# 1/rms by rounded parts, positions behind the low parts, one factor at the end, and a gate moved: four edits to a decoder block on one core

## The chip, the core and the metric

The kernel runs on one core of one Trainium2 chip. The core has a matrix engine (PE, TensorE, whose weight loads the profile shows as PEld), a vector engine (DVE), a scalar engine (ACT), GpSimd (POOL) and a queue for transfers (SP). Each engine works off its own list of instructions in order, and they wait for each other through semaphores. The metric is device time in microseconds (us), the median of three runs of the whole program. All times below are us unless marked ns.

## The reference

One decoder block on 512 tokens of width 1024, in float32. Cut to what matters here:

```python
xn = rmsnorm(x, norm_mix_g)
proj = xn @ w_in     # q latent 384, kv latent 256 + rotary key 32, diff q 512, diff k 512, diff v 512, gates 2 x 1024
# branch A: latent attention, 8 heads (latents normed, projected up, rotary on 32 dims)
# branch B: differential attention, 4 heads of two maps each
o_diff = rmsnorm(softmax(q1 k1) v - lam * softmax(q2 k2) v, g) * (1 - lambda_init)
merged = sigmoid(gate_a) * (o_mla @ w_branch_mla) + sigmoid(gate_b) * (o_diff @ w_branch_diff)
x = x + merged @ w_out
x = x + (silu(hn @ w_gate) * (hn @ w_up)) @ w_down      # hn = rmsnorm(x), hidden width 2816
return rmsnorm(x, norm_final_g)
```

Rotary angles are position times frequency; the kernel turns them into sine and cosine itself.

## The kernel before

**Rounded parts.** Most products on PE are of a rounded float32 format (F32R); line 521 is the one 512-column product of plain float32. To keep accuracy the kernel splits most operands in a high part (rounded, by ACT or DVE) and a low part (the rest, by DVE) and adds three products: high by high, high by low, low by high (`mm3`, lines 299 to 301). Every weight tile is loaded by SP into one of four `raw` buffers (`weights`, line 268), ACT rounds it (line 261) and DVE subtracts (line 266) into one of three `w` buffers. Products gather in PSUM accumulators: three named `mm`, two `sc` (scores), two `tr` (transposes), one `pv` (values).

**Order.** The program is written in a natural order, and a planner puts each engine's instructions in order: it follows a model of their times, takes what is ready by priority, and gives out buffers as they come free. Three priorities are set by hand: attention (`urgent`) goes ahead of the remaining work, and the first reading of a product (`feed`) goes ahead of both. `tc.issue_after(x)` puts an instruction behind `x` on the same engine. The remaining work is filling between the steps of attention; the lists `FILL`, `FILL_MLA` and `FILL_DIFF` (lines 46 to 54) say in which order. An entry is a gate product (24 matmuls of 512 columns, line 468, read out at line 481), `qk` (q and k of a differential head, 24 such matmuls each, lines 568 to 589), `v` (half of the differential values, four groups of 24 matmuls of 256 columns, line 594), or a part of branch A. `FILL_DIFF[0]` stands ahead of differential head 0 in the program.

**Stages.** (1) The start: transposed x, 128 of its 1024 columns at a time, and the latent weights come in; ACT makes the high parts (lines 344, 349) and DVE the low parts (345, 350), while PE multiplies (`latent`). `last_hi` and `last_lo` chain these on ACT and DVE. The positions come over ACT's queue; DVE turns them into angles (401 to 403) and reduces these to parts of a turn (405 to 421), ACT takes sines (433). (2) 1/rms of each token, `x_rs` (four columns of 128 tokens), comes from sums of squares. The gates and the differential q and k have tokens along the free dimension, so they need it as a row repeated on all partitions, `x_rms`: DVE scales an identity by each column (`diag`, 519), PE multiplies a matrix of ones by it (521), DVE copies the result (523). The first gate (line 524) and the cosine and sine tables (538, 540) are multiplied by it. (3) Latents, up-projections, and attention with filling. In `rotate` (555) DVE reads the accumulator twice (shuffle 558, product 559), after which it is free; POOL does the rest (560, 561). (4) Sigmoids, branch and output projections, FFN. (5) The down projection gathers 512 of 1024 output columns for four rows of tokens at a time. `finish` (924) adds the residual (929), ACT sums squares (930), POOL multiplies by the gain (931). After the second half, ACT makes y, an approximate 1/rms, DVE one correction factor z (937, 938), and each half of the row is multiplied by y and by z: the second half on DVE in one instruction (941), the first by y on ACT (940) and by z on DVE (943). SP stores both.

Of the kernel before, what the change touches and what calls it, by code (L numbers as in the profile page):

```python
# [13 lines left out]
F32R = mybir.dt.float32r  # L14
BF16 = mybir.dt.bfloat16
I32 = mybir.dt.int32
AF = mybir.ActivationFunctionType
ALU = mybir.AluOpType
# [3 lines left out]
P = 128  # L22
S = 512
D = 1024
KD = D // P
NB = S // P
# [21 lines left out]
            [("mqk", 2), ("mr", 2), ("gate", 0, 3), ("gate", 0, 4), ("mv", 1)],  # L48
            [("mqk", 3), ("mr", 3), ("qk", 0)],
            [("qk", 1)]]  # L50
FILL_DIFF = [[("qk", 2), ("v", 1)],
             [("qk", 3), ("gate", 0, 5), ("gate", 0, 6)],
             [("gate", 0, 7), ("gate", 1, 0), ("gate", 1, 1)],
             [("gate", 1, m) for m in range(2, KD)]]
PBUFS = dict(mm=3, sc=2, tr=2, pv=1)
# [33 lines left out]
def build(ctx, nc, tc, a, out):  # L89
    sb = ctx.enter_context(tc.tile_pool(name="sb", bufs=1))  # L90
# [8 lines left out]
    def T(tag, shape, dtype):  # L99
        return sb.tile(shape, dtype, name=nm(tag), tag=tag, bufs=BUFS[tag])  # L100

    def PS(tag):
        return pp.tile([P, 512], F32, name=nm("ps_" + tag), tag=tag, bufs=PBUFS[tag])
# [7 lines left out]
    def tmp():  # L111
        return T("t", [P, S], F32)

    def sm(w=1):
        return T("sm", [P, w], F32)

    def r32(ap):
        return ap.bitcast(F32)

    def dma(o, i):  # L120
        nc.sync.dma_start(out=o, in_=i)
# [19 lines left out]
    def urgent():  # L141
        return attention
# [14 lines left out]
    def log_exp(**kw):  # L157
        with tc.issue_after(table[0].ins):
            return nc.scalar.activation(**kw)  # L159
# [12 lines left out]
            nc.tensor.matmul(out=warm_ps, lhsT=warm[:, :P], rhs=warm, start=True, stop=True)  # L172
    ones = sb.tile([P, P], F32, name="ones")
    nc.vector.memset(ones, 1.0)

    misc = T("PT", [P, 2560], F32)

# [14 lines left out]
    ang, turn, pos_i, ah = [misc[:, i * P:(i + 1) * P] for i in (6, 7, 8, 10)]  # L192
    pos_i, ah = pos_i.bitcast(I32), ah.bitcast(F32R)
# [18 lines left out]
    for t in range(NB):  # L212
# [4 lines left out]
                            scalar2=None, op0=ALU.mult)  # L217

    ident = sb.tile([P, P], F32, name="ident")
# [8 lines left out]
    def rsqrt(ss, n, w=1):  # L228

        v, y, z = sm(w), sm(w), sm(w)  # L230
        nc.vector.tensor_scalar(out=v, in0=ss, scalar1=1.0 / n, scalar2=EPS, op0=ALU.mult, op1=ALU.add)
        log_exp(out=y, in_=v, func=AF.Ln)
        last_exp[0] = log_exp(out=y, in_=y, func=AF.Exp, scale=-0.5)
        if w == 1:
            nc.vector.tensor_scalar(out=z, in0=v, scalar1=y, scalar2=y, op0=ALU.mult, op1=ALU.mult)
        else:
            nc.vector.tensor_mul(out=z, in0=y, in1=y)
            nc.vector.tensor_mul(out=z, in0=z, in1=v)
        nc.vector.tensor_scalar(out=z, in0=z, scalar1=-0.5, scalar2=1.5, op0=ALU.mult, op1=ALU.add)
        nc.vector.tensor_mul(out=y, in0=y, in1=z)  # L240
        return y
# [14 lines left out]
    last_hi, last_lo = [None], [None]  # L256
# [69 lines left out]
    lat_mm = [None]  # L326
# [57 lines left out]
    x_rs = rsqrt(x_ss, D, NB)  # L384
# [13 lines left out]

    nc.vector.tensor_copy(out=ang, in_=pos_i)
    nc.vector.tensor_scalar(out=ang, in0=ang, scalar1=ccol[:, 0:1], scalar2=0.0, op0=ALU.mult, op1=ALU.add)
    nc.vector.tensor_copy(out=ah, in_=ang)
    ahl, acc, ry, rx = [v[:, c:c + 2 * P].rearrange("p (s n) -> p s n", s=2) for v in (tmp(), tmp()) for c in (0, 2 * P)]
    with tc.issue_after(last_lo[0].ins):
        nc.vector.tensor_copy(out=ahl[:, 0, :], in_=r32(ah))
    nc.vector.tensor_sub(out=ahl[:, 1, :], in0=ang, in1=ahl[:, 0, :])
    for j, c in enumerate(_inv_2pi_pieces()):
        nc.vector.tensor_scalar(out=ry, in0=ahl, scalar1=c, scalar2=MAGIC, op0=ALU.mult, op1=ALU.add)
# [18 lines left out]
    for src in (turn_c, turn):  # L428
        tg = tmp()
        nc.gpsimd.memset(tg, 0.0)  # L430
        for q in range(4):
            with tc.issue_after(last_sin.ins):
                last_sin = nc.scalar.activation(out=tg[32 * q:32 * q + 32, q * P:(q + 1) * P],
                                                in_=src[32 * q:32 * q + 32, :], func=AF.Sin, scale=TWO_PI)
# [57 lines left out]
    qk = {}  # L492

    def fill(work):
        for kind, *args in work:
            if kind == "gate":
                gate(*args)
            elif kind == "v":
                diff_v(*args)
            elif kind == "qk":  # L500
                qk[args[0]] = diff_qk(*args)
            elif kind == "pe":
                pe[args[0]] = mla_pe(*args)
            elif kind == "mv":
                mv[args[0]] = mla_v(*args)
            elif kind == "mqk":
                mqk[args[0]] = mla_qk(*args)
            elif kind == "mr":
                mla_rope(args[0], mqk[args[0]], pe[args[0] // 2])
# [4 lines left out]
    latent_out(1, pss)  # L514

    ps = PS("mm")
    diag = tmp()
    for t in range(NB):
        nc.vector.tensor_scalar(out=diag[:, t * P:(t + 1) * P], in0=ident, scalar1=x_rs[:, t:t + 1], scalar2=None, op0=ALU.mult)
    with tc.issue_after(lat_mm[0].ins):  # L520
        nc.tensor.matmul(out=ps, lhsT=ones, rhs=diag, start=True, stop=True)
    x_rms = sb.tile([P, S], F32, name="x_rms")
    nc.vector.tensor_copy(out=x_rms, in_=ps)
    gate(0, 0, first_gate)
# [141 lines left out]
        return ps  # L666


    ones_r = sb.tile([P, P], F32R, name="ones_r")
    nc.vector.tensor_copy(out=ones_r, in_=ones)  # L670
    eps = sb.tile([P, 1], F32, name="eps")
    nc.gpsimd.memset(eps, EPS)

# [137 lines left out]
    for h in range(4):  # L811
        parts_first[0] = True
        fill(FILL_DIFF[h])
        with urgent():
# [50 lines left out]
    for t, half in ((0, 0), (1, 0), (0, 1), (1, 1), (2, 0), (2, 1), (3, 0), (3, 1)):  # L865
        xs = x1[t][:, half * S:(half + 1) * S]
        ps = PS("mm")
# [16 lines left out]
    for f, n in products[:3]:  # L884
        w = weights(kview(n, f * P, P), KD, P)
        ps = PS("mm")
# [4 lines left out]
    for n_, (f, n) in enumerate(products):  # L891
        if n_ < 3:
            ps, w = early[n_]
            ffn_product(ps, w, 256, 512)
        else:
            w = weights(kview(n, f * P, P), KD, P)
            ps = PS("mm")
# [26 lines left out]
    def finish(t, c0, c1, ps):  # L924

        xs = x1[t][:, c0:c1]
        g = g_fin[c0 // S][:, c0 % S:c0 % S + c1 - c0]
        ss, b = sm(), sm()
        nc.vector.tensor_add(out=xs, in0=xs, in1=ps)
        nc.scalar.activation(out=tmp()[:, :c1 - c0], in_=xs, func=AF.Square, accum_out=ss)  # L930
        nc.gpsimd.tensor_mul(out=xs, in0=xs, in1=g)  # L931
        nc.vector.tensor_scalar(out=b, in0=ss, scalar1=1.0 / D, scalar2=base.get(t, EPS), op0=ALU.mult, op1=ALU.add)
        if c1 == D:
            y, z = sm(), sm()
            log_exp(out=y, in_=ss, func=AF.Ln, scale=1.0 / D, bias=base[t])
            log_exp(out=y, in_=y, func=AF.Exp, scale=-0.5)
            nc.vector.tensor_scalar(out=z, in0=b, scalar1=y, scalar2=y, op0=ALU.mult, op1=ALU.mult)
            nc.vector.tensor_scalar(out=z, in0=z, scalar1=-0.5, scalar2=1.5, op0=ALU.mult, op1=ALU.add)
            xs, x0 = x1[t][:, S:D], x1[t][:, 0:S]
            nc.scalar.activation(out=x0, in_=x0, func=AF.Copy, scale=y)  # L940
            nc.vector.tensor_scalar(out=xs, in0=xs, scalar1=y, scalar2=z, op0=ALU.mult, op1=ALU.mult)
            dma(out[0, t * P:(t + 1) * P, S:D], xs)
            nc.vector.tensor_scalar(out=x0, in0=x0, scalar1=z, scalar2=None, op0=ALU.mult)
            dma(out[0, t * P:(t + 1) * P, 0:S], x0)
        base[t] = b

    for half in range(2):
        acc = [PS(t_) for t_ in (("mm", "mm", "mm", "sc") if half == 0 else ("sc", "tr", "tr", "pv"))]

        def down(t, w, k0):  # L950
            for k in range(2):
                mm3(acc[t], [hid[k0 + k][s][:, t * P:(t + 1) * P] for s in range(2)],
                    [w[s][:, k, :] for s in range(2)], k0 + k == 0, k0 + k == NF - 1)

        last = []
        for k0 in range(0, NF, 2):
            w = weights(kview("w_ffn_down", half * S, S, k0, 2), 2, S)
            if half == 1 and k0 >= NF - 6:
                last.append((w, k0))
                continue  # L960
            for t in range(NB):
                down(t, w, k0)
        for t in range(NB):
            for w, k0 in last:
                down(t, w, k0)
            for c0, c1 in (((0, LAST), (LAST, S)) if half == 1 and t == NB - 1 else ((0, S),)):
                finish(t, half * S + c0, half * S + c1, acc[t][:, c0:c1])
# [32 lines left out]
```

## Time and profile before

| what | value |
|---|---|
| three runs | 740.13, 741.04, 740.1; median 740.13 |
| the profiled execution, its own time | 740.23 |
| span from first to last instruction in it | 738.5 |
| mean granted PE clock | 0.999 |

The span of the profiled execution is 1.7 shorter than its own time; the rest lies around the span. The profile has these views: a page with busy times, the chain that ended last and the costliest groups; waits (who waited for whom); a timeline of instructions (start, duration, engine, line, operation, output and inputs, shapes, count, and in brackets idle time ahead of it with what ended it); and busy time by stretches. Matmuls overlap and their ends are modelled, so a step from one start to the next says more than a duration.

### The profile page before, as it was taken

Reading aid. Unit: us, or ns where it says so; the run is one execution under the profiler, and the core shown is the slowest. Engines: PE = TensorE matmul, PEld = TensorE weight load, DVE = VectorE, ACT = ScalarE, POOL = GpSimd, SP = SyncE. Lnnn points to the kernel's source line nnn. Section 1 sums busy time; section 2 is a strip of 40 time slices with the busy share of each in tenths; the row PEclk is TensorE's granted clock in tenths of the full one; section 3 lists DMA queues with packets and bytes.
Section 4 is the critical chain, followed back from the end, with each engine's and each line's share of the span. In section 5 each row is a group of like instructions: output and inputs, shape, how many; then the busy total and the mean of one; then the engine's idle time right before and its main releaser. Section 6 shows DMA issues by size and latency. Waiting matters only on the chain.

```text
span 738.5 us, 9543 instructions
## 1 busy us (share of the span) xinstructions
PE 729.0 (99%) x3602; PEld 617.2 (84%) x3602; DVE 413.6 (56%) x812; ACT 333.7 (45%) x613; POOL 48.4 (7%) x45
## 2 busy tenths in 40 slices
PE   9999999999999999999999999999999999999996
PEld 7978988888888888888898888888888888888885
DVE  7789789988898765793634333333233232222514
ACT  7765678676766526561433223223232231212314
POOL 1000000322041101000000000000000000000303
PEclk9999999999999999999999999999999999999999
DMA  9615455323433312346204233332333323223203
GB/s 335 196 59 138 120 129 137 93 59 85 115 86 86 114 59 87 114 161 210 84 3 143 86 108 92 90 110 86 105 94 88 112 86 102 98 88 113 86 1 114
DMA packets 100414, 78.82 MB, mean 107 GB/s; under 512 B 6416, under 2 KB 87056, under 8 KB 100368
## 3 DMA queue, kind: packets, MB, share of 16 engines
q1 hardware_dynamic: 100080, 78.13, 35.9%
q8 instruction: 28, 0.46, 0.3%
q14 instruction: 18, 0.15, 0.1%
q10 hardware_dynamic: 288, 0.08, 0.0%
HBM read 71.91 MB, written 2.10 MB: 100 GB/s over the span
## 4 chain that ended last, share of the span: by engine, by line
PE 96%; DVE 3%; ACT 0%; issue 0%; DVEq 0%
PE ps_mm L299 25%; PE ps_mm L300 25%; PE ps_mm L301 25%; PE ps_sc L627 3%; PE ps_tr L653 2%; PE ps_tr L301 2%; PE ps_sc L300 2%; PE ps_sc L299 2%; PE ps_sc L301 2%; PE ps_tr L299 2%; PE ps_tr L300 2%; PE ps_pv L774 1%; PE ps_pv L664 1%; PE ps_pv L301 1%; PE ps_pv L300 1%; PE ps_pv L299 1%
## 5 line engine op out<-in xcount | busy, mean ns | idle before, releaser
L261 ACT ACTIVATE w<-raw 128x1024 fp32r<-128x1024 f32 (+3 forms) x110 | 109.4, 998 | 253.5 <-issue 150.7
L266 DVE TENSOR_TENSOR w<-raw,w 128x1024 fp32r<-128x1024 f32 (+3 forms) x114 | 133.7, 1175 | 159.8 <-ACT w L261 159.5
L299 PE MATMUL ps_mm<-X,w 128*128 128x512 f32 (+1 forms) x568 | 217.3, 383 | 0.1
L300 PE MATMUL ps_mm<-X,w 128*128 128x512 f32 (+1 forms) x568 | 216.8, 382 | 0.0
L301 PE MATMUL ps_mm<-X,w 128*128 128x512 f32 (+1 forms) x568 | 216.4, 381 | 0.0
L299 PEld LDWEIGHTS ps_mm<-X,w 128*128 128x128 f32 x568 | 106.7, 188 | 20.4 <-issue 0.3
L300 PEld LDWEIGHTS ps_mm<-X,w 128*128 128x128 f32 x568 | 106.9, 188 | 20.0 <-issue 0.2
L301 PEld LDWEIGHTS ps_mm<-X,w 128*128 128x128 f32 x568 | 106.8, 188 | 20.0
L905 DVE TENSOR_TENSOR t<-t,ps_mm 128x512 f32<-128x512 f32 x22 | 15.1, 688 | 66.8 <-PE ps_mm L301 66.1
L159 ACT ACTIVATE P<-P,sm 128x128 f32<-128x128 f32 (+3 forms) x64 | 35.7, 558 | 21.4 <-DVE sm L631 21.0
L931 POOL TENSOR_TENSOR L<-L,P 128x512 f32<-128x512 f32 (+1 forms) x9 | 12.6, 1421 | 434.8 <-ACT t L930 434.8
L627 PE MATMUL ps_sc<-L,L 96*128 96x128 f32 (+7 forms) x160 | 37.3, 327 | 0.2 <-DVE sm L631 0.2
L300 PE MATMUL ps_mm<-w,L 128*128 128x512 f32 (+1 forms) x100 | 37.3, 373 | 0.0
L299 PE MATMUL ps_mm<-w,L 128*128 128x512 f32 (+1 forms) x100 | 37.1, 373 | 0.0
L301 PE MATMUL ps_mm<-w,L 128*128 128x512 f32 (+1 forms) x100 | 37.0, 373 | 0.0
L300 PE MATMUL ps_mm<-L,w 128*128 128x512 f32 x90 | 35.4, 394 | 0.0
L299 PE MATMUL ps_mm<-L,w 128*128 128x512 f32 x90 | 35.4, 395 | 0.0
L301 PE MATMUL ps_mm<-L,w 128*128 128x512 f32 x90 | 35.1, 390 | 0.0
L631 DVE CUSTOM_DVE_ANT_0 P<-ps_sc,mask 128x128 f32<-128x128 f32 (+3 forms) x64 | 30.5, 477 | 5.8 <-PE ps_sc L627 5.0
L246 ACT ACTIVATE L<-t 64x512 fp32r<-64x512 f32 (+2 forms) x47 | 29.2, 621 | 6.9 <-PE ps_pv L301 3.7
L627 PEld LDWEIGHTS ps_sc<-L,L 96*128 96x128 f32 (+1 forms) x160 | 26.7, 189 | 3.3 <-DVE sm L631 0.4
L250 DVE TENSOR_TENSOR L<-t,L 128x512 fp32r<-128x512 f32 (+2 forms) x37 | 26.3, 711 | 3.5 <-ACT L L246 3.1
(271 smaller groups left out, 1136.8 us busy)
## 6 DMA issues: line engine op xcount, KB each, us to landing
raw<-w_in SPq DMA_DIRECT2D x28, 512.0 KB, 4.0
raw<-w_ffn_gate SPq DMA_DIRECT2D x22, 512.0 KB, 3.9
raw<-w_ffn_up SPq DMA_DIRECT2D x22, 512.0 KB, 3.9
raw<-w_ffn_down SPq DMA_DIRECT2D x22, 512.0 KB, 3.6
L<-x SPq DMA_DIRECT2D x8, 512.0 KB, 7.3
L<-L SPq DMA_DIRECT2D x32, 128.0 KB, 3.7
raw<-w_out SPq DMA_DIRECT2D x8, 512.0 KB, 3.9
L<-xt SPq DMA_DIRECT2D x8, 256.0 KB, 4.4
```

Of the source, the lines that this page charges most:

```text
L159: return nc.scalar.activation(**kw)
L246: nc.scalar.activation(out=hi, in_=src, func=AF.Copy, scale=scale)
L250: nc.vector.tensor_sub(out=lo, in0=src, in1=r32(hi))
L261: nc.scalar.activation(out=o, in_=i, func=AF.Copy)
L266: (nc.vector if w_eng[1] == 'dve' else nc.gpsimd).tensor_sub(out=o, in0=i, in1=r32(hi))
L299: nc.tensor.matmul(out=o, lhsT=lh, rhs=rh, start=start, stop=False)
L300: nc.tensor.matmul(out=o, lhsT=lh, rhs=rl, start=False, stop=False)
L301: return nc.tensor.matmul(out=o, lhsT=ll, rhs=rh, start=False, stop=stop)
L627: nc.tensor.matmul(out=ps[:, :n], lhsT=q[:, i * P:n], rhs=k[:, 0:n], start=j == 0, stop=j == last)
L631: nc.vector.tensor_tensor_reduce(out=m, in0=ps[:, :n], in1=mask[:, S - n:], scale=-1.0, scalar=3.4e38, op0=ALU.add, op1=ALU.min, accum_out ...
L653: nc.tensor.transpose(out=ps[:, c:c + P], in_=blocks[i][:, j * P:(j + 1) * P], identity=ident)
L905: nc.vector.tensor_mul(out=g, in0=g, in1=ps)
```

## The change

Four edits. 1/rms as a row: `x_rs` is split in a rounded part and the rest, each gives a diagonal, and two products with a rounded matrix of ones (`ones_r`, now made at the start) replace the one product of plain float32. Positions: the copy that begins the angles is put behind the last low part (`last_lo`), and the rounded copy of the angles behind it follows by its inputs. The end: DVE multiplies y and z once into yz; each half of the row is multiplied by yz, the first on ACT, which also issues the store of it on its own queue, the second on DVE, stored by SP. Filling: gate 5 of the first branch moves from the second list of `FILL_DIFF` to the head of the first one, ahead of `qk 2`.

```diff
-FILL_DIFF = [[("qk", 2), ("v", 1)],
-             [("qk", 3), ("gate", 0, 5), ("gate", 0, 6)],
+FILL_DIFF = [[("gate", 0, 5), ("qk", 2), ("v", 1)],
+             [("qk", 3), ("gate", 0, 6)],
              [("gate", 0, 7), ("gate", 1, 0), ("gate", 1, 1)],
...
+    ones_r = sb.tile([P, P], F32R, name="ones_r")
+    nc.vector.tensor_copy(out=ones_r, in_=ones)
...
-    nc.vector.tensor_copy(out=ang, in_=pos_i)
+    with tc.issue_after(last_lo[0].ins):
+        nc.vector.tensor_copy(out=ang, in_=pos_i)
...
-    with tc.issue_after(last_lo[0].ins):
-        nc.vector.tensor_copy(out=ahl[:, 0, :], in_=r32(ah))
+    nc.vector.tensor_copy(out=ahl[:, 0, :], in_=r32(ah))
...
-    diag = tmp()
-    for t in range(NB):
-        nc.vector.tensor_scalar(out=diag[:, t * P:(t + 1) * P], in0=ident, scalar1=x_rs[:, t:t + 1], scalar2=None, op0=ALU.mult)
-    with tc.issue_after(lat_mm[0].ins):
-        nc.tensor.matmul(out=ps, lhsT=ones, rhs=diag, start=True, stop=True)
+    x_hi, x_lo = sm(NB), sm(NB)
+    nc.vector.tensor_copy(out=x_hi.bitcast(F32R), in_=x_rs)
+    nc.vector.tensor_sub(out=x_lo, in0=x_rs, in1=x_hi)
+    for j, part in enumerate((x_hi, x_lo)):
+        diag = tmp().bitcast(F32R)
+        for t in range(NB):
+            nc.vector.tensor_scalar(out=diag[:, t * P:(t + 1) * P], in0=ident, scalar1=part[:, t:t + 1], scalar2=None,
+                                    op0=ALU.mult)
+        with tc.issue_after(lat_mm[0].ins):
+            nc.tensor.matmul(out=ps, lhsT=ones_r, rhs=diag, start=j == 0, stop=j == 1)
...
-            nc.scalar.activation(out=x0, in_=x0, func=AF.Copy, scale=y)
-            nc.vector.tensor_scalar(out=xs, in0=xs, scalar1=y, scalar2=z, op0=ALU.mult, op1=ALU.mult)
+            nc.vector.tensor_mul(out=yz, in0=y, in1=z)
+            nc.scalar.activation(out=x0, in_=x0, func=AF.Copy, scale=yz)
+            nc.scalar.dma_start(out=out[0, t * P:(t + 1) * P, 0:S], in_=x0)
+            nc.vector.tensor_scalar(out=xs, in0=xs, scalar1=yz, scalar2=None, op0=ALU.mult)
             dma(out[0, t * P:(t + 1) * P, S:D], xs)
-            nc.vector.tensor_scalar(out=x0, in0=x0, scalar1=z, scalar2=None, op0=ALU.mult)
-            dma(out[0, t * P:(t + 1) * P, 0:S], x0)
```

More of the change, by code (lines that the diff above doesn't have):

```diff
@@ L666, in values @@
         return ps
-    ones_r = sb.tile([P, P], F32R, name="ones_r")
-    nc.vector.tensor_copy(out=ones_r, in_=ones)
     eps = sb.tile([P, 1], F32, name="eps")
@@ L933, in finish @@
         if c1 == D:
-            y, z = sm(), sm()
+            y, z, yz = sm(), sm(), sm()
             log_exp(out=y, in_=ss, func=AF.Ln, scale=1.0 / D, bias=base[t])
```

## The prediction, made before the result was known

> **What bounds the kernel now.** I read the head of the page first, then TensorE's own waits, then a table by stretches of time, and last the single instructions around each hole.
>
> ```profile
> span 738.5 us, 9543 instructions
> PE 729.0 (99%) x3602; PEld 617.2 (84%) x3602; DVE 413.6 (56%) x812; ACT 333.7 (45%) x613; POOL 48.4 (7%) x45
> ...
> PE 96%; DVE 3%; ACT 0%; issue 0%; DVEq 0%
> ```
>
> The last row is the chain that ended last: 96% of it is TensorE (PE). So only two things can shorten the run: fewer PE columns, or the holes in which PE waits. The 3% of VectorE (DVE) says where to look for the holes. TensorE's waits name one, and the table by stretches shows the stage that it lies in (columns: busy time and count of PE, PEld, DVE, ACT, POOL, then granted clock, DMA share and GB/s).
>
> ```profile
> PE ps_mm L299 <- DVE t L559: 0.9, 1, 0.9
> ```
>
> ```profile
> 160.00:177.00 17.00, 17.00 (x113) 15.69 (x113) 13.38 (x33) 12.51 (x27) 3.79 (x4) 1.00 0.39 94
> 177.00:196.00 19.00, 17.69 (x108) 14.95 (x108) 18.74 (x47) 14.24 (x32) 5.68 (x4) 1.00 0.25 58
> ...
> 276.00:731.00 455.00, 454.97 (x2092) 379.94 (x2091) 179.95 (x233) 145.78 (x210) 13.77 (x9) 1.00 0.32 97
> ```
>
> From 276 on PE is never without work, so what is gained or lost ahead of it arrives at the end in full. Between 177 and 196 DVE is busy 18.74 of 19 us and PE is not. That is where differential head 0 runs, with the third head's q and k (line 51, `qk 2`) and the second value half (`v 1`) as filling. The instructions:
>
> ```profile
> 42.11 0.40 PE L301 MATMUL ps_mm<-X,w 128*128 128x512 f32 x1
> 42.34 0.39 PE L299 MATMUL ps_mm<-X,w 128*128 128x512 f32 x1
> ...
> 167.11 0.39 PE L301 MATMUL ps_mm<-X,w 128*128 128x512 f32 x1
> ...
> 179.45 0.28 PE L653 MATMUL ps_tr<-ident,P 128*128 128x128 f32 x1
> 179.91 0.44 PE L627 MATMUL ps_sc<-L,L 128*128 128x128 f32 x2 [0.18 <-DVE sm L631]
> 181.21 0.39 PE L299 MATMUL ps_mm<-w,X 128*128 128x256 f32 x1 [0.86 <-DVE t L559]
> ...
> 193.73 0.51 PE L627 MATMUL ps_sc<-L,L 128*128 128x384 f32 x2
> 194.46 0.82 PE L664 MATMUL ps_pv<-PT,L 128*128 128x512 f32 x2 [0.22 <-ACT PT L246]
> 195.33 0.50 PE L299 MATMUL ps_mm<-X,w 128*128 128x512 f32 x1
> ```
>
> ```profile
> 179.85 0.74 DVE L558 STREAM_SHUFFLE t<-ps_mm 128x512 f32<-128x512 f32 x1
> 180.48 0.68 DVE L559 TENSOR_TENSOR t<-ps_mm,tab 128x512 f32<-128x512 f32 x1
> ...
> 181.72 0.67 DVE L559 TENSOR_TENSOR t<-ps_mm,tab 128x512 f32<-128x512 f32 x1
> ```
>
> The ends of matmuls are modelled, so I use starts. A 512-column matmul starts 0.23 after the one before it (42.11 to 42.34), a 128-column one by that scale 0.06. The step from 179.45 to 179.91 is 0.46 instead of 0.06, hole A of 0.40. From 179.91 to 181.21 pass 1.30 instead of 0.12, hole B of 1.18. At 193.73 two of 384 columns should take 0.34 and take 0.73; at 194.46 one of 512 and one of 384 should take 0.40 and take 0.87: hole C, 0.39 + 0.47 = 0.86. The reason of B is in the rows: the k product of `qk 2` was complete at 167.11, yet its rotation (L558, L559), which frees the accumulator, ends at 182.39, 15 us later, and that of q ends at 181.16. The three `mm` accumulators are then q, k and the first half of `v 1`; the second half starts at 181.21, when q's is read out.
>
> **Part 1, 1/rms by rounded parts.** Removed: one 128x512 product of plain float32. Added: two of rounded parts, and on DVE a rounding copy, a subtraction and four more diagonal blocks.
>
> ```profile
> 40.78 1.02 PE L521 MATMUL ps_mm<-t,ones 128*128 128x512 f32 x2
> ...
> 41.87 0.40 PE L300 MATMUL ps_mm<-X,w 128*128 128x512 f32 x1
> ```
>
> From 40.78 to 41.87 pass 1.09; the one ordinary matmul left out between them is 0.23 of that, so L521 costs 0.86. Two rounded products, by the ordinary step, cost 2 x 0.23 = 0.46, a saving of 0.40 on PE. Whether it arrives depends on DVE:
>
> ```profile
> 34.13 0.17 DVE L386 TENSOR_TENSOR sm<-sm 128x4 f32<-128x4 f32 x1
> ...
> 34.41 0.28 DVE L519 TENSOR_SCALAR t<-ident,sm 128x128 f32<-128x128 f32 x1
> 36.17 0.43 DVE L436 CAST P<-t 128x512 fp32r<-128x512 f32 x1 [1.48 <-ACT t L433]
> ...
> 47.33 0.69 DVE L481 TENSOR_TENSOR L<-ps_mm,x_rms 128x512 f32<-128x512 f32 x1 [0.71 <-PE ps_mm L301]
> ```
>
> ```profile
> 49.89 0.47 PE L299 MATMUL ps_mm<-L,w 128*128 128x512 f32 x1
> 50.46 0.66 PE L460 MATMUL ps_tr<-ident,L 128*128 128x128 f32 x4
> ```
>
> By the first two rows the addition is 2 x 0.17 + 4 x 0.28 = 1.5 us at most, nearer 1.2 where such instructions overlap. Two idle times cover it: 1.48 ahead of L436, if the blocks are placed there, and 0.71 ahead of L481. PE stands 0.34 at 49.89 (0.57 instead of 0.23) at the end of the DVE work that L481 begins, so the saving lives only if L481 starts earlier too. Bounds: -0.4 with DVE covered, +0.5 if all 1.2 falls behind 36.17 and only 0.7 is covered. I take -0.3, near the first, because 2.2 of cover stand against 1.2.
>
> **Part 2, positions behind the low parts.** Three small DVE instructions leave the start and run just ahead of the angle reduction.
>
> ```profile
> 4.45 0.23 DVE L401 CAST PT<-PT 128x128 f32<-128x128 int32 x1 [0.46 <-DMA PT<-positions]
> ...
> 5.18 0.75 DVE L345 SCALAR_TENSOR_TENSOR X<-L,cols,X 128x512 fp32r<-128x512 f32 x1
> ...
> 29.51 0.17 DVE L231 TENSOR_SCALAR sm<-sm 128x4 f32<-128x4 f32 x1 [1.83 <-ACT L L379]
> ```
>
> From L401 to the first low part (L345) pass 0.73, and the low parts move up by about that; but PE is still on high parts then and has no wait there among its waits. Where they go, the angle chain ends ahead of an idle 1.83, and 0.7 fits. I cost it at 0; if the cover were gone it would be +0.7 of DVE time with the 0.71 ahead of L481 still behind it. No DMA moves.
>
> **Part 3, one factor at the end.**
>
> ```profile
> 732.17 0.42 ACT L930 ACTIVATE t<-L 128x256 f32<-128x256 f32 x1 [1.71 <-DVE L L929]
> ...
> 733.73 0.72 ACT L940 ACTIVATE L<-L,sm 128x512 f32<-128x512 f32 x1
> 733.98 0.15 DVE L938 TENSOR_SCALAR sm<-sm 128x1 f32<-128x1 f32 x1
> 734.24 0.55 DVE L941 TENSOR_SCALAR L<-L,sm,sm 128x512 f32<-128x512 f32 x1
> 734.70 0.48 DVE L943 TENSOR_SCALAR L<-L,sm 128x512 f32<-128x512 f32 x1
> 734.82 0.81 SPq L121 DMA_DIRECT2D out<-L  x2
> ```
>
> ```profile
> 736.00:736.50 0.50, 0.00 (x0) 0.00 (x0) 0.00 (x0) 0.00 (x0) 0.00 (x0) 1.00 0.98 369
> ```
>
> The product y*z (0.17, by L386, with its wait 0.2) comes ahead of both scalings. The one-factor form takes 0.48 instead of 0.55, so the first store leaves some 0.1 later. ACT's copy of the other half no longer runs under z but behind y*z: 734.45 to 735.17, and its store is issued then, about where SP issues its second one today (734.82 plus half of 0.81). The DMA engines are at a share of 0.98 while both stores drain, so the end follows the first store: +0.1. For the earlier rows of tokens ACT now also spends some 0.4 per store issue, and its Square of the next rows (L930) is queued behind. Before the last L930 ACT idles 1.71; a copy some 0.65 later plus 0.4 fits. Bounds: -0.4 (one issue time, if the issue were what delays the last store) and +0.5 (an ACT that comes late to L930).
>
> [...]
>
> **Part 4, a gate ahead of `qk 2`.** The sum of PE work is unchanged: 24 matmuls of 0.23, 5.5 us, move from behind `qk 3` to ahead of `qk 2`, with one weight load (on SP's queue, now ahead of those of `qk 2`, `v 1` and `qk 3`, in a ring of four raw buffers), ACT's high part, DVE's low part and the read-out L481. Behind the gate's old place the order is as before. PE now reaches the second half of `v 1` 5.5 us later relative to the heads, some 185.6 instead of 180.1, while q's rotation ends at 181.16 if DVE keeps its place for it. Then B is gone, and A too, since there is filling between the transposes and the scores again. C waits for ACT's probabilities and for `v 1`'s read-out in a full DVE queue, which I leave as it is. So -1.5 of A + B = 1.58, keeping 0.1 for ordinary hand-over. Bounds: -2.4 (all three), and +1.9 (rival below).
>
> **Sum**: -0.3 + 0 + 0.1 - 1.5 = -1.7, against the profiled execution's own 740.23 (its span and 1.7 around it), which is 0.1 over the median of 740.13: **738.5**.
>
> **Rivals.** *The rotation moves along* (or the planner puts the gate elsewhere). q's and k's read-out may be late because their inputs and buffers are late, and then the hole follows them to 186. For it: 15 us of delay is no matter of one product. Against it: both rotations stand back to back in DVE's order, as if they had waited for one thing. Then only parts 1 and 3 count: 740.0.
>
> *All holes close.* The gate's DVE work goes into the 3.6 us that DVE idles between 160 and 177, and the full stretch is thinned by what moves behind it. A + B + C with part 1: -2.4 - 0.3 + 0.1 = -2.6, 737.6. Against it: C sits in head 0's own chain.
>
> *DVE pays for the gate inside the full stretch*, the slower side. Its low part and read-out then take their place between 177 and 196, where DVE has 0.26 us left:
>
> ```profile
> L266 DVE TENSOR_TENSOR w<-raw,w 128x1024 fp32r<-128x1024 f32 (+3 forms) x114 | 133.7, 1175 | 159.8 <-ACT w L261 159.5
> ```
>
> ```profile
> 183.24 3.18 POOL L561 TENSOR_TENSOR t<-t,t 128x512 f32<-128x512 f32 x2
> ...
> 183.57 1.69 DVE L681 SCALAR_TENSOR_TENSOR P<-P,sm,P 128x384 f32<-128x384 f32 x1
> ```
>
> 1.18 + 0.69 = 1.9 later for every softmax step behind it, A and B staying: 740.23 - 0.2 + 1.9 = 741.9. It decides once the gate's L266 starts after 177. The second fence shows why the stretch is tight: a mix of 384 columns takes 1.69 beside POOL's addition, more than three times the 0.48 of a 512-column scaling at 734.70.
>
> [...]
>
> **Numbers.** Forecast 0.42 (its own range 738.0 to 739.2), all holes close 0.23, the rotation moves along 0.20, DVE pays 0.15. A measurement here tells 0.2%, 1.48 us, from no change, so faster means below 738.65: 0.26 of the forecast's share and all of the second, 0.49. Slower means above 741.61: the last case, 0.15. Same: 0.16 of the forecast and the 0.20, 0.36. The range of 737.2 to 741.2 goes from all holes closed with the full 0.4 of part 1 up to the last case, most of which it leaves out.
>
> **What would show it.** Right: the step that starts `v 1`'s second half has no wait; L521's successor stands 0.46 behind it; PE's hole near 50 is no larger than 0.34; the last store's drain begins 0.1 later after the last matmul. Wrong: a wait of `ps_mm` on L559 near 186; a gate's L266 inside the full stretch; ACT at L930 after the sums are ready; new PE waits of over 0.5 anywhere between 195 and 276, where there is none now.

## The result and the profile after

The changed kernel takes **747.22 us** (median of 4 runs, 747.04 to 747.37) against 740.12 (a fourth run of the kernel before is counted in; 740.09 to 741.04): a ratio of 1.0092, 95% interval 1.008 to 1.0104. It is 7.1 us slower, where the forecast was 738.5 and its range ended at 741.2.

The head of the page and the chain that ended last, changed kernel:

```profile
span 745.6 us, 9555 instructions
PE 730.6 (98%) x3602; PEld 618.3 (83%) x3602; DVE 412.2 (55%) x818; ACT 333.5 (45%) x613; POOL 48.4 (6%) x45
...
PE 90%; ACT 4%; DVE 4%; issue 1%; DMA 0%; ACTq 0%; DVEq 0%; SPq 0%
```

TensorE (PE) does the same 3602 matmuls, so the 7.1 us between the spans (745.6 and 738.5) are waits and matmuls that ran slower. TensorE's waits, changed kernel (what waited, on whom, us in total, times, longest):

```profile
PE ps_mm L301 <- DVE L L797: 3.7, 1, 3.7
...
PE ps_sc L634 <- DMA L<-L: 0.7, 1, 0.7
PE ps_mm L301 <- DVE t L566: 0.7, 1, 0.7
PE ps_tr L462 <- DVE L L254: 0.4, 1, 0.4
```

Lines moved by 2 to 7: L301 was L299, L566 was L559, L634 was L627, L797 was L792. The first wait is new, and by far the largest. The same table by stretches as before, with the last stretch cut up (busy time and count of PE, PEld, DVE, ACT, POOL, then granted clock, DMA share, GB/s), changed kernel:

```profile
160.00:177.00 17.00, 17.00 (x93) 14.59 (x92) 12.48 (x28) 9.92 (x19) 4.91 (x4) 1.00 0.39 94
177.00:196.00 19.00, 18.35 (x138) 17.41 (x137) 17.09 (x44) 13.88 (x32) 5.04 (x4) 1.00 0.21 50
276.00:289.00 13.00, 13.00 (x63) 10.90 (x62) 5.33 (x7) 1.09 (x2) 1.30 (x1) 1.00 0.27 81
289.00:297.00 8.00, 4.26 (x12) 3.10 (x11) 3.78 (x6) 7.77 (x12) 1.26 (x1) 0.79 0.21 67
297.00:737.60 440.60, 440.57 (x2029) 368.06 (x2027) 171.43 (x220) 135.87 (x196) 11.04 (x7) 1.00 0.31 97
```

Between 177 and 196 PE is busier than before (18.35 against 17.69 us) and VectorE (DVE) less full (17.09 against 18.74), as the forecast wanted. The loss stands in the row 289 to 297, a stretch that was full before: PE works 4.26 of 8 us, and with a granted clock of 0.79. Its single instructions:

```profile
289.20 0.39 PE L303 MATMUL ps_mm<-L,w 128*128 128x512 f32 x1
293.33 0.73 PE L301 MATMUL ps_mm<-L,w 128*128 128x512 f32 x1 [3.74 <-DVE L L797]
293.86 0.63 PE L302 MATMUL ps_mm<-L,w 128*128 128x512 f32 x1
...
296.42 0.59 PE L302 MATMUL ps_mm<-L,w 128*128 128x512 f32 x1
296.84 0.40 PE L303 MATMUL ps_mm<-L,w 128*128 128x512 f32 x1
297.08 0.39 PE L301 MATMUL ps_mm<-L,w 128*128 128x512 f32 x1
```

Two things are to be seen. From 289.20 to 293.33 pass 4.13 instead of 0.23: a hole of 3.9. And the steps behind it are 0.43 (0.53 for the first) until 296.84: from 293.33 to 297.08 pass 3.75 for nine matmuls that should take 2.05, so 1.7 more go to the clock: the granted share is 0.50 from 293.4 to 296.8 and 1.00 from 297 on. L797 multiplies the first branch product by its sigmoid gate and so frees an accumulator; without it the fourth product can't begin. Why is it late? ScalarE (ACT), changed kernel first, then the kernel before:

```profile
289.17 0.69 ACT L159 ACTIVATE t<-ps_tr,eps 128x512 f32<-128x512 f32 x1 [7.14 <-PE ps_tr L704]
...
291.83 2.56 ACT L490 ACTIVATE L<-L,cols 128x512 f32<-128x512 f32 x4
```

```profile
284.02 0.69 ACT L159 ACTIVATE t<-ps_tr,eps 128x512 f32<-128x512 f32 x1 [6.75 <-PE ps_tr L699]
...
286.69 2.56 ACT L488 ACTIVATE L<-L,cols 128x512 f32<-128x512 f32 x4
```

The sigmoids stand behind the Ln and Exp of the last differential head's norm (L159). That norm comes 5.1 us later, and the sigmoids with it. In the kernel before, the same hand-over had almost no room (VectorE, then TensorE):

```profile
287.44 0.69 DVE L792 TENSOR_TENSOR L<-L,ps_mm 128x512 f32<-128x512 f32 x1 [1.34 <-ACT L L488]
```

```profile
288.81 0.39 PE L299 MATMUL ps_mm<-L,w 128*128 128x512 f32 x1
```

L792 ended at 288.13 and the fourth product began at 288.81: 0.7 us of cover, and the change took 5.

Two more places lost time. The first is a wait before 70 us on the first transfers of the rotated keys. The queues and transfers issued between 66 and 68.9 us (packets, MB and share of the DMA engines; then KB and median us from issue to landing), changed kernel, then the kernel before:

```profile
q8 instruction: 1, 0.02, 2.2%
q14 instruction: 1, 0.01, 0.7%
...
L<-L SPq DMA_DIRECT2D x3, 128.0 KB, 3.2
```

```profile
L<-L SPq DMA_DIRECT2D x4, 128.0 KB, 2.3
```

Two fetches of code (the rows of kind instruction, queues q8 and q14) fall into this stretch, where the kernel before has none, and the transfers land after 3.2 us instead of 2.3. The second place is the end; ScalarE, then VectorE, changed kernel:

```profile
738.43 0.42 ACT L935 ACTIVATE t<-L 128x256 f32<-128x256 f32 x1 [1.75 <-DVE L L934]
...
738.89 0.72 ACT L946 ACTIVATE L<-L,sm 128x512 f32<-128x512 f32 x1
739.52 0.40 ACT L935 ACTIVATE t<-L 128x256 f32<-128x256 f32 x1
```

```profile
737.98 0.75 DVE L934 TENSOR_TENSOR L<-L,ps_pv 128x256 f32<-128x256 f32 x2 [0.80 <-PE ps_pv L303]
738.64 0.15 DVE L945 TENSOR_TENSOR sm<-sm,sm 128x1 f32<-128x1 f32 x1
```

The scaling of the third token block (L946) sits between the two squares (L935) of the fourth, because its factor y*z (L945) is made behind the fourth block's additions (L934). Before, the two squares started 0.42 apart (732.17 and 732.59); now it is 1.09.

Following the start of the k-th matmul in both kernels, changed less before, the 7.1 us divide thus: +0.1 from the start, +0.1 from part 1 by 52 us, **+0.9** at 70 us, -0.5 in the stretch of part 4 by 287 us, **+5.65** between 289 and 297 (3.9 of wait, 1.7 of clock), **+0.84** behind the last matmul.

### The profile page after: what moved, and what is told of

Its sections match the earlier page's. It is cut to its first block, busy times and chain, and to the rows that moved or that the text cites. A ratio compares the mean times of both kernels' runs of the same rounds, so it can differ in the third digit from the quotient of the medians.

```text
span 745.6 us, 9555 instructions
## 1 busy us (share of the span) xinstructions
PE 730.6 (98%) x3602; PEld 618.3 (83%) x3602; DVE 412.2 (55%) x818; ACT 333.5 (45%) x613; POOL 48.4 (6%) x45
## 3 DMA queue, kind: packets, MB, share of 16 engines
q10 hardware_dynamic: 864, 1.13, 0.4%
## 4 chain that ended last, share of the span: by engine, by line
PE 90%; ACT 4%; DVE 4%; issue 1%; DMA 0%; ACTq 0%; DVEq 0%; SPq 0%
PE ps_mm L301 24%; PE ps_mm L302 24%; PE ps_mm L303 23%; PE ps_sc L634 3%; PE ps_tr L660 2%; PE ps_sc L301 1%; PE ps_sc L303 1%; PE ps_tr L303 1%; PE ps_tr L301 1%; PE ps_tr L302 1%; PE ps_sc L302 1%; PE ps_pv L779 1%; PE ps_pv L671 1%; PE ps_pv L301 1%; DVE w L268 1%
## 5 line engine op out<-in xcount | busy, mean ns | idle before, releaser
L301 PE MATMUL ps_mm<-X,w 128*128 128x512 f32 (+1 forms) x568 | 216.5, 382 | 0.3 <-DVE L L254 0.3
L301 PEld LDWEIGHTS ps_mm<-X,w 128*128 128x128 f32 x568 | 106.7, 188 | 20.9 <-DVE L L254 0.5
L159 ACT ACTIVATE P<-P,sm 128x128 f32<-128x128 f32 (+3 forms) x64 | 35.8, 560 | 27.6 <-DVE sm L638 27.3
L301 PE MATMUL ps_mm<-L,w 128*128 128x512 f32 x90 | 36.1, 403 | 3.7 <-DVE L L797 3.7
L634 PE MATMUL ps_sc<-L,L 96*128 96x128 f32 (+7 forms) x160 | 37.6, 327 | 0.8 <-DMA L<-L 0.7
L301 PE MATMUL ps_mm<-w,L 128*128 128x512 f32 (+1 forms) x100 | 37.1, 373 | 0.0
L302 PE MATMUL ps_mm<-L,w 128*128 128x512 f32 x90 | 36.0, 400 | 0.0
L303 PE MATMUL ps_mm<-L,w 128*128 128x512 f32 x90 | 35.6, 396 | 0.0
L634 PEld LDWEIGHTS ps_sc<-L,L 96*128 96x128 f32 (+1 forms) x160 | 26.4, 190 | 4.1 <-DMA L<-L 1.0
```

The source lines that it names most:

```text
L301: nc.tensor.matmul(out=o, lhsT=lh, rhs=rh, start=start, stop=False)
L302: nc.tensor.matmul(out=o, lhsT=lh, rhs=rl, start=False, stop=False)
L303: return nc.tensor.matmul(out=o, lhsT=ll, rhs=rh, start=False, stop=stop)
L634: nc.tensor.matmul(out=ps[:, :n], lhsT=q[:, i * P:n], rhs=k[:, 0:n], start=j == 0, stop=j == last)
```

## The experiments

All ratios are to the kernel before, timed on the same chip in the same rounds.

**Parts alone.** Three kernels carry one part each, one carries all but the gate.

```diff
-FILL_DIFF = [[("qk", 2), ("v", 1)],
-             [("qk", 3), ("gate", 0, 5), ("gate", 0, 6)],
+FILL_DIFF = [[("gate", 0, 5), ("qk", 2), ("v", 1)],
+             [("qk", 3), ("gate", 0, 6)],
```

> Only the moved gate, everything else as before. Theory: the moved gate is what loses the time. Its 24 products stand ahead of work that attention needs, so the last normalisation's Ln comes some 5 us later, the sigmoids with it, and PE, which has no filling left, waits 3 to 4 us for the first merge behind the sigmoids near 289 us and then runs some matmuls at half clock: 744.5 to 746 (about 5 us above before). Rival A (the prediction's part 4): holes A and B close and nothing else moves, 738.5 to 739. Rival B: the loss needs parts 1 to 3 as well, 739 to 741.

Measured: 745.9 against 740.23, ratio 1.0074 (1.0061 to 1.0086). The gate alone loses 5.7 us, by the same wait (TensorE's waits, then ScalarE, then the stretch; gate alone):

```profile
PE ps_mm L299 <- DVE L L792: 3.7, 1, 3.7
```

```profile
288.16 0.69 ACT L159 ACTIVATE t<-ps_tr,eps 128x512 f32<-128x512 f32 x1 [7.17 <-PE ps_tr L699]
```

```profile
289.00:297.00 8.00, 4.68 (x14) 3.72 (x15) 3.78 (x6) 7.97 (x13) 1.26 (x1) 0.79 0.15 53
```

The norm comes 4.1 us later than before (288.16 against 284.02), while the filling ends 0.4 earlier (matmul number 1560 of the run, counted from 0, starts at 287.04 instead of 287.45). The wait follows: 4.1 + 0.4 - 0.7 of cover = 3.8. The 4.1 can be counted: the last matmul that this norm needs (L699, a product with a matrix of ones) was number 1543 in PE's order and is now number 1563, so 20 of the gate's 24 matmuls have come ahead of it. That is 4.5 us, of which the closed holes gave 0.4 back.

The changed kernel with the gate put back:

> The changed kernel with the gate put back to where it was (parts 1, 2 and 3 remain). Theory: no wait over 1 us near 289 us; what is left is +0.1 of parts 1 and 2, about +0.9 if the transfers of the rotated keys at 68 us still land late, and +0.8 at the end: 741 to 742. Rival B (the loss comes from parts 1 to 3): 744 or more. The prediction's sum for these three parts (-0.3, 0, +0.1) gives 739.9.

Measured: 741.34, ratio 1.0014 (1.0005 to 1.0023). No wait is left near 289. Parts 1 to 3 together are 1.1 slower, not 0.2 faster; that is 0.5 less than parts 1 and 3 lose singly below, and the profiled execution is 0.7 ahead by 11 us, where a hole of 0.5 near 6 us, seen in the other two, is missing. There PE waits for the first low part, which part 2 moves ahead (see part 2 further below).

Part 3 alone:

> Only the last scaling by one factor with its second queue (part 3). Theory: ScalarE's scaling of the third token block is put between the two squares of the last block, because VectorE's product of the two factors stands behind the last block's additions; the end comes 0.7 to 0.9 later: 740.8 to 741.1. The prediction's term: +0.1, 740.2, if that order on ScalarE came only from the other parts' shift.

Measured: 741.15, ratio 1.001 (1.0002 to 1.0019): +0.9, and the last matmul starts when it did before. Part 1 alone:

> Only the rounded parts of 1/rms with the earlier copy of the ones (part 1). Theory: the plain matmul's 0.4 us goes, and the copy of the broadcast is put behind the first latent norm, so that PE stands 0.4 to 0.6 us longer before 50 us: 740.1 to 740.4 if the transfers near 68 us land as before, 740.9 to 741.2 if their delay comes with this part. The prediction's term: -0.3, 739.8.

Measured: 740.97, ratio 1.0008 (0.9999 to 1.0017): +0.7. The transfers near 68 us are late in it too (2.9 against 2.3), with a PE wait of 0.6 on them.

**Is it the accumulator, and is it the clock?** Two edits of the changed kernel. The first lets two early branch products use the score buffers:

```diff
-            ps = PS("mm")
+            ps = PS(tags[i])
...
-        branch(0, m, o_mla)
+        branch(0, m, o_mla, {2: ("mm", "sc"), 4: ("sc", "mm")}.get(m, ("mm", "mm")))
```

> The changed kernel with two of the first branch products accumulating in the score buffers, idle by then, so that PE needs the first merged gate only for its sixth product and not for its fourth. Theory (PE waits near 289 us only for an accumulator that the sigmoid's merge holds, and the half clock follows from that wait): the wait of 3.9 and the slow matmuls behind it go, 741.3 to 742.0. Rival: the sigmoids are late against all the branch products and the wait only moves to a later product, 745 to 747.

Measured: 741.06 against 740.50, ratio 1.0009 (1.0001 to 1.0018), 6.2 below the changed kernel. Of that, 5.65 is this stretch: between 288 and 297 us the distance to the kernel before, matmul by matmul, no longer grows. The rest is a start that was 0.7 quicker in the profiled execution. The stretch in this kernel:

```profile
289.00:297.00 8.00, 8.00 (x37) 6.63 (x36) 4.97 (x8) 7.94 (x13) 1.29 (x1) 1.00 0.20 66
```

PE is full and its clock 1.00, though the norm ahead of the sigmoids still comes at 288.52, earlier than in the changed kernel only by the quicker start. The second edit fills the wait with 16 matmuls:

```diff
+            if lead == (m, i):
+                dps = PS("sc")
+                for d in range(16):
+                    with tc.issue_after(last_br[0].ins):
+                        last_br[0] = nc.tensor.matmul(out=dps, lhsT=ones_r, rhs=o[d % 4][:, 0, :], start=True, stop=True)
```

> The changed kernel with 16 added matmuls (128x512, about 0.23 us each, 3.65 us in all) into a score buffer behind the third branch product, in the place of the wait near 289 us; their result isn't used. Theory: the wait's length stays, but the nine matmuls behind it run in 0.23 instead of 0.43 us, 745.1 to 745.6: 1.9 of the loss belongs to the clock and 3.9 to the wait. Rival: the half clock has another cause than the idle stretch, 747.2 or more.

Measured: 745.36, ratio 1.0066 (1.0052 to 1.008), 1.9 below the changed kernel although 16 matmuls were added:

```profile
289.24 3.79 PE L799 MATMUL ps_sc<-L,ones_r 128*128 128x512 f32 x16
293.15 0.50 PE L301 MATMUL ps_mm<-L,w 128*128 128x512 f32 x1
293.49 0.40 PE L302 MATMUL ps_mm<-L,w 128*128 128x512 f32 x1
```

The fourth product still begins at 293.15, but behind a first step of 0.34 the steps are 0.23 to 0.24. The granted clock of 289 to 297 is 1.00 in this run, where it was 0.79 with PE idle: here the half clock came with the idle PE. The nine matmuls that took 3.75 us now take 2.21: the clock costs 1.5 to 1.7 on top of the wait, and 0.2 of the 1.9 was won before 70 us.

**Part 3 for the last token block alone.** The kernel before, with the new form only where t is the last block:

```diff
+            if t < NB - 1:
+                nc.scalar.activation(out=x0, in_=x0, func=AF.Copy, scale=y)
...
+            else:
+                nc.vector.tensor_mul(out=yz, in0=y, in1=z)
+                nc.scalar.activation(out=x0, in_=x0, func=AF.Copy, scale=yz)
+                nc.scalar.dma_start(out=out[0, t * P:(t + 1) * P, 0:S], in_=x0)
```

> The kernel before with part 3 (one factor, second queue) for the last token block alone; the other three blocks are scaled as before. Theory: 0.1 later than before for the product of the two factors, 740.2 to 740.5, because the third block's scaling on ScalarE no longer waits for a product behind the last block's additions. Rival: the loss of 0.9 lies in the last block itself (second queue, its store), 741.1.

Measured: 740.37 against 740.50, ratio 1.0001 (0.9992 to 1.0009). ScalarE at the end, part 3 alone and then this kernel:

```profile
732.63 0.72 ACT L941 ACTIVATE L<-L,sm 128x512 f32<-128x512 f32 x1
733.26 0.40 ACT L930 ACTIVATE t<-L 128x256 f32<-128x256 f32 x1
```

```profile
732.59 0.40 ACT L930 ACTIVATE t<-L 128x256 f32<-128x256 f32 x1
```

The second square is back at 732.59, and only the span's +0.1 (738.6 against 738.5) is left. Of part 3's loss, 0.7 was the third block's scaling in the fourth block's way.

**Part 1 and the fetch of code.** Part 1 adds six VectorE instructions. The kernel before gets six that do nothing of use, ahead of all data; the order of everything else is the same on every engine.

```diff
+    pad = sb.tile([P, 1], F32, name="pad")
+    for _ in range(6):
+        nc.vector.memset(pad, 1.0)
```

> The kernel before with six added VectorE memsets of 128x1 at the start, ahead of any data; the order of all other instructions is the same on every engine. Theory (part 1 lost 0.8 us because its six more VectorE instructions bring VectorE's next fetch of code some 3 us earlier, onto the first transfers of the rotated keys): the fetch comes near 68.5 us, PE waits 0.7 to 0.9 before 70 us, 740.8 to 741.1. Rival (the fetch has nothing to do with it): 740.1 to 740.3, and the transfers land in 2.3 us as before.

Measured: 741.56, ratio 1.0012 (1.0004 to 1.0021). The fetch came at 68.7, the first two transfers landed after 3.4 and 3.1 us, and PE stood 0.8 behind 69.67. But 1.1 was lost, more than that. The counter-test takes part 1 and moves the fetch away:

> Part 1 alone, with ten added VectorE memsets of 128x1 at the start, so that VectorE's fetch of code comes ahead of the first transfers of the rotated keys instead of among them; the order of everything else is that of part 1 alone. Theory: the 0.8 us lost before 70 us comes back, 740.0 to 740.4. Rival (the transfers are late for another effect of part 1): 740.9 to 741.2, and they land late again.

Measured: 741.12, ratio 1.0008 (1.0 to 1.0017): a miss. The fetch came at 60.8, the transfers landed in 2.3 us and the wait was gone, and yet nothing was gained. The loss had come in elsewhere, with the memsets' own tile. It was separated by writing the memsets into the tile of ones, `nc.vector.memset(ones[:, 0:1], 1.0)`, so that no new tile is needed:

> The kernel before with six VectorE memsets of 128x1 at the start that write into the tile of ones; no tile moves. Theory: the fetch falls on the first transfers of the rotated keys and costs 0.8 to 0.95, 740.9 to 741.2, without the slower matmuls that the earlier run had. Rival (the tile did it all): 740.1 to 740.4.

Measured: 741.02, ratio 1.001 (1.0001 to 1.0018).

> Part 1 alone with ten VectorE memsets of 128x1 at the start that write into the tile of ones, so that no tile moves in SBUF. Theory (fetch and layout are two separate costs): the transfers land as before, no wait before 70 us, no slower matmuls near 612 us, 740.1 to 740.5. Rival (the fetch only moves the loss elsewhere): 740.9 to 741.3.

Measured: 740.20 against 740.18, ratio 1.0 (0.9991 to 1.0009). The queues and transfers between 66 and 68.9 us in these two, six memsets first:

```profile
q8 instruction: 1, 0.02, 2.2%
q14 instruction: 1, 0.01, 0.7%
...
L<-L SPq DMA_DIRECT2D x3, 128.0 KB, 3.1
```

```profile
L<-L SPq DMA_DIRECT2D x4, 128.0 KB, 2.3
```

Six idle instructions in the kernel before cost the 0.8 us that part 1 costs; part 1 with the fetch out of the way (61.0) costs nothing that can be measured: the wait of 0.4 on VectorE's L256 (L254 in the changed kernel) stands against the 0.4 saved. The tile alone:

> The kernel before with one tile of 128x1 and one memset into it: every later tile lies 4 bytes further in SBUF or more, and VectorE's fetch of code moves by one instruction only. Theory: the matmuls that read the PT tile step 0.017 us slower, 0.4 to 0.6 in all, 740.6 to 740.9. Rival (the layout doesn't matter): 740.1 to 740.3.

Measured: 740.75 against 740.18, ratio 1.0011 (1.0002 to 1.0021). The matmuls that take the first two hidden blocks from the long PT tile, one row of the groups between 600 and 700 us, the kernel before and then with the tile (busy, mean ns):

```profile
L301 PE MATMUL ps_sc<-w,PT 128*128 128x512 f32 x4 | 1.6, 389 | 0.0
```

```profile
L304 PE MATMUL ps_sc<-w,PT 128*128 128x512 f32 x4 | 1.6, 396 | 0.0
```

From start to start these take 233.0 ns instead of 226.7, while the same matmuls with hidden blocks from other tiles stay at 226.7. The expectation's 0.017 us was an estimate of the author that no run shows, and it is too large; against the kernel's own steps it is 0.006 us, 48 times, 0.3 us. Another 0.24 is lost between 330 and 390 us, 0.13 of it on 24 matmuls that read tiles named PT as their moving side.

**What is the gate worth, and do the repairs add up?** The gate with the two score buffers, without parts 1 to 3:

> The kernel before with the moved gate and with two of the first branch products in the score buffers: the gate without the wait near 289 us. It tells what closing holes A and B is worth. Theory: part of them opens again at 185 and 200 us, so that about 0.4 of the 1.5 is left as a gain, 739.6 to 740.0. Rival (the prediction's part 4 holds once the late wait is gone): 738.5 to 739.0.

Measured: 739.75 against 740.23, ratio 0.9993 (0.9984 to 1.0002): 0.5 of gain, which the times alone don't tell from nothing. The traces do: from 160 to 287 us, matmul by matmul, this kernel, the gate alone, the changed kernel and the one with the look-ahead each win 0.4 to 0.5. All three repairs on the changed kernel, first with the memsets' own tile, then without:

> The changed kernel with all three repairs: two branch products in the score buffers, ten added VectorE memsets of 128x1 at the start, and one factor with the second queue for the last token block alone. Theory (the three losses are separate and add up): 741.1 of the first repair alone, less 0.9 near 70 us, less 0.7 at the end, 739.3 to 739.7. Rival (they share a cover, or the fetch hits another transfer): 740 to 741.

Measured: 740.11, ratio 0.9999 (0.999 to 1.0008).

> The changed kernel with the three repairs (two branch products in the score buffers, ten VectorE memsets at the start, now into the tile of ones, one factor with the second queue for the last token block alone). Theory: 0.5 below the same kernel with a tile of its own for the memsets, 739.4 to 739.8. Rival: 740.0 or more, the repairs don't add up.

Measured: 739.87 against 740.18, ratio 0.9995 (0.9986 to 1.0003). The repairs add up: the profiled execution is 7.8 shorter than that of the changed kernel, 0.55 of it by a quicker start and 7.3 by the repairs (5.65, 0.9 and 0.7). But they only bring the change back to where it started: no version here is faster than the kernel before by more than the measurement tells. One more attempt held the second latent norm behind the copy of 1/rms, to recover part 1's 0.4:

> The same with the second latent norm held until the copy of the broadcast 1/rms, so that this copy runs near 44 us as before and not behind the norm. Theory (part 1 lost its 0.4 us to that order on VectorE): 0.4 below the kernel with the three repairs, 738.9 to 739.4. Rival: the transposes of the last latents wait for the norm instead, no gain or 0.5 to 1.5 slower.

Measured: 743.01 (740.84 to 743.57), ratio 1.0028 (1.0019 to 1.0038). The planner then arranged the work behind it in another order, and a rotation became late instead (TensorE's waits, then the stretch behind this wait, which ends at 60.96):

```profile
PE ps_mm L304 <- DVE t L570: 2.3, 1, 2.3
```

```profile
61.60:65.20 3.60, 3.60 (x11) 2.79 (x10) 3.54 (x7) 1.16 (x2) 0.00 (x0) 0.53 0.15 28
```

Behind this wait, too, PE's clock is low: 0.53 over these 3.6 us.

## Why the prediction was wrong

**Part 4, forecast -1.5, measured +5.7.** The failing step is the sentence "From 276 on PE is never without work, so what is gained or lost ahead of it arrives at the end in full". It took the full stretch as a property of the stage. It was full because the sigmoids came 0.7 us before they were needed. The working counted what the gate's 5.5 us did to the hole, and that "the sum of PE work is unchanged", but not what stands behind it in PE's order: attention, its last norm, and the sigmoids. In the gate alone, 20 of the 24 moved matmuls came ahead of what that norm needs: 4.5 us, less the 0.4 of closed holes, against 0.7 of cover. The look-ahead in the score buffers shows that nothing else is in it: with two more accumulators the late sigmoids hold nothing up.

The gain itself was also mis-sized: it is 0.5 (the gate with the look-ahead, and the shift of 0.5 by 287 us), not 1.5. Hole A went. Of B 0.87 came back at 186.36 as the wait on L566, which the prediction had named as a sign against itself. Its condition "if DVE keeps its place for it" had failed: the first of the two rotations ended at 187.23, not at 181.16. And C's 0.86 became 1.35 at 200 to 202 us. If every step between 177 and 210 us that is over 0.1 longer than its columns take is counted, the holes were 2.88 and are 2.44. So the rival that *the rotation moves along* was half right in the place, and no rival had the mechanism that decided. *DVE pays for the gate* did forecast slower, but from a fuller VectorE; VectorE became less full there (17.09 of 19 us).

**The clock** was in no term: a wait of 3.9 us costs 5.6 in the changed kernel.

**Part 1, forecast -0.3, measured +0.7.** The saving on PE is as worked out; TensorE, changed kernel:

```profile
40.87 0.40 PE L528 MATMUL ps_mm<-t,ones_r 128*128 128x512 f32 x1
41.11 0.40 PE L301 MATMUL ps_mm<-X,w 128*128 128x512 f32 x1
```

The step is 0.24 where L521 took 0.86 for its one product; with the second product 0.4 are saved. But the condition "the saving lives only if L481 starts earlier too" was not met. VectorE, changed kernel and before:

```profile
46.49 0.68 DVE L530 COPY x_rms<-ps_mm 128x512 f32<-128x512 f32 x1
```

```profile
43.17 0.68 DVE L523 COPY x_rms<-ps_mm 128x512 f32<-128x512 f32 x1
```

The eight diagonal blocks were placed just ahead of the first latent norm, not in the idle time of 1.48, and the copy fell behind both norms. That cost the 0.4 again (the wait on L254). The bound of +0.5 held for this. The other 0.8 came from the fetch of code, of which the prediction had nothing.

**Part 2, forecast 0**, wasn't run alone, but the traces speak for a gain. The first matmuls run slowly for a time that differs between executions: the first three high products take 1.31 us in the kernel before (from 5.08 to 6.39), 0.62 in part 3 alone. Where they run fast, PE needs the first low part sooner; part 3 alone, then the changed kernel with the gate put back, which has part 2:

```profile
5.67 0.34 PE L299 MATMUL ps_pv<-L,X 128*128 128x384 f32 x1
6.46 0.45 PE L300 MATMUL ps_mm<-L,X 128*128 128x384 f32 x1 [0.45 <-DVE L L350]
```

```profile
5.63 0.34 PE L301 MATMUL ps_pv<-L,X 128*128 128x384 f32 x1
5.84 0.44 PE L302 MATMUL ps_mm<-L,X 128*128 128x384 f32 x1
```

Eight of the eleven traces without part 2 have this wait (0.2 to 0.6), none of the seven with it. By 11 us the four fast starts with part 2 are 0.5 to 0.7 ahead of the kernel before; every trace without it lies between 0.1 ahead and 0.3 behind. So the step "PE is still on high parts then and has no wait there among its waits" held for the one execution that was read, a slow start, and the term of 0 left out some 0.6 that a fast start gains. The changed kernel's profiled execution is a slow start, too, and shows +0.1.

**Part 3, forecast +0.1, measured +0.8.** The last block by itself is +0.1, as worked out. The failing step is "Before the last L930 ACT idles 1.71; a copy some 0.65 later plus 0.4 fits". The idle time is there still (1.75 ahead of L935), but the copy doesn't go into it: its factor is made on VectorE behind the fourth block's additions, so it comes 0.46 after that idle time has ended. The bound of +0.5 had named an ACT that comes late to L930, but too small. The working looked at ScalarE's cover and not at the queue of the engine that feeds it. The term counted no gain from the second queue, and none was measured: with that queue in the last block alone the ratio is 1.0001 (0.9992 to 1.0009).

**What was right**: that A closes, the 0.4 of L521, the +0.1 of y*z, that the second queue was counted at no gain, and that VectorE doesn't pay for the gate.

## What to carry to other kernels

A stretch without waits is not a stretch with room: before work is moved ahead of a chain, find the next hand-over of that chain to the busy engine and write down its margin (here 288.13 against 288.81). A filling moved forward delays what stands behind it in an in-order queue by its own length, less the holes that it closes (here 4.5 - 0.4 = 4.1), and that has to fit into the margin. For the small terms, look at who produces the operand of a moved instruction, and at what chance adds: here 0.8 us from where code is fetched, 0.5 from where tiles lie and 0.5 to 0.7 from how the first microseconds go. Six empty instructions and one empty tile showed the first two; for the third, compare starts before totals.

## What was not expected of the hardware

- After PE stood for 3.9 us, nine matmuls ran at steps of 0.43 instead of 0.23, and the granted clock was 0.50 from 293.4 to 296.8 (0.79 over 289 to 297). In the same kernel, steps of 0.79, 0.99 and 0.92 at 48.88, 69.74 and 186.36 left it at 1.00, and so did one of 1.13 at 180.08 in the kernel before. Filling the wait with 16 matmuls kept it at 1.00. Steps of 0.43 also followed a shorter wait, in the last attempt above: there PE stood for 2.7 us (58.28 to 60.96), and its steps from 61.80 to 64.78 are 0.43. Waits of a length between 1.13 and 2.7 weren't tried.
- Transfers beside a fetch of code landed later. In the kernel before, fetches begin at 71.12 (16 KB, q8) and 71.76 (8 KB, q14): the transfers of rotated keys issued at 69.78, 70.42 and 71.05 land after 4.0, 3.8 and 3.6 us, the five ahead of them after 2.2 to 2.3. In the changed kernel the fetches begin at 67.79 and 68.79: those issued at 66.72, 67.44 and 68.07 land after 3.3, 3.2 and 3.0, the five behind them after 2.3 to 2.4. Six VectorE instructions at the start moved the fetch onto the first transfers (3.1 against 2.3 above). The 8 KB fetch that matters here begins when 193 VectorE instructions of the trace, waits counted, have begun in the kernel before, 192 in the changed kernel; a later one (122.76 and 119.80) behind 321 and 320. The 16 KB fetch does not always fall with it: in part 1 alone none is seen between 65.8 and 70 us, and the wait on the transfers was 0.6 all the same. What sets the time of a fetch stays open.
- One tile of 4 bytes a partition, allocated first, made the 48 matmuls that take their stationary side from the PT tile 6 ns (3%) slower each (233.0 instead of 226.7), 24 that stream such a tile 5 ns, and the run 0.5 us in all. What it is in the layout that decides wasn't tried.
